# Block products for the feed-forward input projections: 44 of 88 column pairs in seven half-size products

## The chip, the core and the metric

The kernel runs on one core of a Trainium2 chip. The time is device microseconds for one execution, from a median of several runs. TensorE (PE) multiplies, VectorE (DVE) and ScalarE (ACT) work elementwise and read the PSUM banks, GpSimd (POOL) works elementwise on SBUF, SyncE (SP) issues the DMA transfers. Each engine executes its own list of instructions in order and waits for others by semaphores.

## What is computed

The reference is one step of a two-layer streaming encoder for 512 prompt frames and 64 sample frames, 576 tokens of width 1024. Each layer is feed-forward, token mixer, feed-forward, each with a modulated RMS norm in front and a gated residual behind. The change lies in the feed-forwards:

```
def _swiglu(h, w_in, w_out):                       # w_in (1024, 5632), w_out (2816, 1024)
    gate, up = jnp.split(h @ w_in, 2, axis=-1)
    return (jax.nn.silu(gate) * up) @ w_out

mod = (cond @ ada_w[l] + ada_b[l]).reshape(b, N_SUB, 3, D_MODEL)     # the modulation vectors of a layer
```

There are four feed-forwards: 0 ahead of and 1 behind the mixer of layer 0, 2 and 3 around that of layer 1. 1, 2 and 3 are called F1, F2 and F3. All is float32.

## The kernel before, in words

Tokens lie along the free dimension, in two halves of 288 (`HALF`). Features lie in partitions, 8 tiles of 128. A float32 product is made of three passes: each operand is split into a high part, its copy in the fp32r type, and a low part, the rest; a weight tile `wh`, `wl` and an activation `XH`, `XL` give wh x XH + wh x XL + wl x XH, three matmuls of 128x128 weights on 288 tokens each.

`plan` (line 49) lists the weight tiles in order of use, as pairs of blocks. A feed-forward goes in three chunks of 8, 8 and 6 column tiles (`CHUNKS`). Of each column tile j a pair holds the gate's block and the up projection's block, 8 weight tiles of 128x128 each, one DMA of 512 KB per block. After the input pairs of a chunk come its output products. `dense` (379) issues a pair: for either half of the tokens, for gate and up, 8 contraction tiles of 3 matmuls: 96 matmuls. A gate or up tile of a half has a PSUM bank of its own from a ring of four, `d`. `evac` in `ffn` (645) takes them out: silu of the gate to `sg` on ScalarE, product `hm` on VectorE, its split into `HH` (ScalarE) and `HL` (VectorE).

The weights come through a ring of three `stage` buffers. `w_prep` (364) splits a block: `wh` on ScalarE, `wl` on VectorE, each 128x1024, and then issues the transfer of the next block (`w_dma`, 354). `dense` calls it for the next pair's first block at the start of the first half and for its second block at the start of the second half, before that half's matmuls; `wh` and `wl` have rings of four.

The order of all instructions is settled while the program is written. `Model` (111) keeps rough times of the engines from fixed costs, and `Sched` (242) holds background tasks, generators that yield the time at which they are due. After every three matmuls `mm` calls `S.tick()`, which runs every task whose time has come on the model's TensorE clock (a 288-column matmul counts 123 ns there); what it issues stands in each engine's list at that place. `finish` (278) runs a task to its end at once.

`start_sub` (629) issues the first two pairs of a feed-forward, first halves first, while the norm of the second half is still worked out on VectorE, ScalarE and GpSimd. `last_pairs` (606) does the last output products, residuals and the next norm. `ada_task` (585) makes the modulation vectors of layer 1 in the background of F1 and F2: 72 tiles `aw` of 128x1024, each one DMA and two VectorE instructions `jk` with a read of the accumulator, one tile every 8500 ns of the model's clock, later if the model's VectorE is more than that ahead:

```
            for kt in range(8):
                while hold[0]:
                    yield S.clock + 1000.0
                ada_dma(pool, ahead)
                ada_tile(pool, cb, l, j, kt)
                yield max(S.clock + every, M.t["DVE"] - 1000.0)
```

Two tiles are fetched before the loop, so that two are on their way when one is read.

Of the kernel before, what the change touches and what calls it, by code (L numbers as in the profile page):

```python
# [19 lines left out]
F32 = mybir.dt.float32  # L20
# [7 lines left out]
P = 128  # L28
# [4 lines left out]
D = 1024  # L33
# [12 lines left out]
DSH = ((2, 4, 6), (1, 4, 6))  # L46


def plan():
    """The weight tiles in the order in which they are used, as pairs of blocks of up to eight 128 x 128 products;  # L50
    a tile is (source, index, rows, column)."""
# [6 lines left out]
    def ffn(f):  # L58
        for j0, nj in CHUNKS:
            for j in range(j0, j0 + nj):  # L60
                two([("in", f, tuple(range(8)), j * P), ("in", f, tuple(range(8)), FF + j * P)])
# [43 lines left out]
def outs(nk):  # L105
    """The output tiles of each pair of blocks whose sums run over nk products."""
    n = 2 if nk > 4 else (4 if nk > 2 else 8)
    return [tuple(range(m, m + n)) for m in range(0, 8, n)]


class Model:
    """Rough times of the engines, in ns, by which the background work is interleaved with the dense products."""
# [37 lines left out]
    def free(self, key, bufs):  # L150
        """When the ring's next buffer is free."""
# [73 lines left out]
class Ring:  # L225
    """A tile pool whose reuse of buffers the model sees."""
# [15 lines left out]
class Sched:  # L242
    """Interleaves the background work with the stream of dense products."""
# [45 lines left out]
def encoder_step(ctx: ExitStack, tc: tile.TileContext, a, o):  # L289
# [30 lines left out]
    # ---------------------------------------------------------------- constants  # L320
# [26 lines left out]
    # ---------------------------------------------------------------- weights  # L347
# [15 lines left out]

    def w_prep(i, g, E=None):
        if i >= len(pairs) or g >= len(pairs[i]):
            return
# [63 lines left out]

    def dense_first(evacs, feed):
        """The first two pairs of all, step by step for both halves as feed makes their inputs."""
# [36 lines left out]
    # ---------------------------------------------------------------- rsqrt, norms  # L469
# [23 lines left out]
    def norm_r(pool, halves):  # L493
        """1/rms of each token of these halves, tokens in partitions."""
# [61 lines left out]
    # ---------------------------------------------------------------- adaLN vectors  # L556
# [81 lines left out]
    def ffn(l, s, pool, task, out):  # L638
        for ci, (j0, nj) in enumerate(CHUNKS):
            HH = pool.tile([P, 8, NT], F32R, name="HH")  # L640
            HL = pool.tile([P, 8, NT], F32R, name="HL")
            for jj in range(nj):
                gate = {}

                def evac(g, half, ps, jj=jj, gate=gate):
                    t0, t1 = HALF[half]
                    if g == 0:
                        gate[half] = pool.tile([P, 288], F32, name="sg", bufs=2)
# [9 lines left out]
                elif ci == 0 and jj == 1:  # L658
                    if callable(task):
                        dense_first([ev0, evac], task)  # L660
                    else:
                        start_sub(task, [ev0, evac])
                else:
# [9 lines left out]
    # ---------------------------------------------------------------- layer 0 mixer  # L673
    def mixer0(pool, task, npool):
# [111 lines left out]
        def own(p, name, shape, at):  # L786
            """Buffers of a pair of heads; those of pair 2 lie in the residual's, which waits in DRAM."""
# [47 lines left out]
        def gdn_pair(p, kq, vt):  # L835
# [58 lines left out]
            # decay and the matrices within a block  # L894
# [20 lines left out]
            # the sample's block: both heads on the diagonal  # L915
# [20 lines left out]
        def spill(src, dst):  # L936
            """Blocks of 32 from their rows' partitions to one partition each, or back, through DRAM."""
# [34 lines left out]
            # 16 -> 32  # L972
# [18 lines left out]
            # 32 -> 64  # L991
# [19 lines left out]
            # 64 -> 128  # L1011
# [12 lines left out]
        def gdn_chunks(p, ktok, stok, nv, sc, nat, DM, PS):  # L1024
# [9 lines left out]
            # the sample's state step  # L1034
# [9 lines left out]
            # prompt: chunk by chunk  # L1044
# [68 lines left out]
            # norm of the heads' outputs, gate, back to feature-major  # L1113
# [114 lines left out]
    # ---------------------------------------------------------------- layer 1 mixer  # L1228
# [164 lines left out]
    # ---------------------------------------------------------------- the whole step  # L1393
# [13 lines left out]
    with tc.tile_pool(name="ada", bufs=1) as ap, tc.tile_pool(name="ffn", bufs=1) as fp:  # L1407
        ap, fp = Ring(M, ap), Ring(M, fp)
        crow = [ap.tile([P, D], F32, name="awp", bufs=3)[0:1] for _ in range(2)]
# [32 lines left out]
        row = ap.tile([P, D], F32, name="awp", bufs=3)[:, :P]  # L1442
# [15 lines left out]
        def scales(n):  # L1458
            """The modulation's scale for four of the feature tiles, each in a column group of its own."""
# [74 lines left out]
# columns of the packed small vectors  # L1534
# [93 lines left out]
```

## Time and profile before

| what | us |
|---|---|
| median of 3 runs | 2509.28 |
| lowest and highest run | 2495.31, 2509.33 |
| the profiled execution, first to last instruction | 2512.2 |
| F1 in the trace | about 905 to 1301 |
| F2 | about 1336 to 1731 |
| F3 | about 2095 to 2491 |

The profiled execution is one more execution; the page gives its span and nothing around it, so its span is set beside the runs' times. The profile names an instruction by engine, operation, the tiles that it writes and reads (buffer numbers left out) and their shape. Busy time is time in which at least one instruction of an engine is under way; the ends of matmuls are modelled and overlap. All instructions carry one line (188), that of the helper that issues them, so they are told apart by their tiles. PEclk is the granted TensorE clock as a share of full speed.

### The profile page before, as it was taken

To read this page: it belongs to the slowest core of one execution; us is meant where nothing else is said; L and a number is where in the kernel's file an instruction comes from. 1 tells how busy PE (TensorE), PEld (TensorE's weight loads), DVE (VectorE), ACT (ScalarE), POOL (GpSimd) and SP (SyncE) were. 2 spreads that over 40 slices of the span, in tenths; PEclk is the share of its full clock that TensorE was granted. 3 is DMA by queue.
4 is the path that set the end of the run, shared out by engine and by line. 5 is a ranking of instruction groups with operands and counts; after the bars stand their busy time and mean duration, and the time that the engine had idled before them with its cause. 6 is when DMAs were issued, how large, how long until landed. Compare 5 with 4: busy or idle time off the path is not lost.

```text
span 2512.2 us, 46274 instructions
## 1 busy us (share of the span) xinstructions
PE 2430.6 (97%) x19084; PEld 2357.9 (94%) x19084; DVE 1506.0 (60%) x2964; ACT 835.3 (33%) x1571; POOL 354.2 (14%) x599
## 2 busy tenths in 40 slices
PE   6999999999998999999999999999999999999998
PEld 5999999988888999999999999999888889999998
DVE  7677776597785666556556555535555664333334
ACT  4322212543322342122233222124655544222122
POOL 4000000341222220000021000002333332000001
PEclk8999999998877999999999999999999999999999
DMA  6555554321213144444434444322322122322222
GB/s 240 168 162 167 166 165 131 112 75 50 57 46 98 56 154 143 134 136 144 130 105 135 142 129 141 110 76 85 100 74 84 53 73 91 85 77 84 85 78 70
DMA packets 95399, 277.04 MB, mean 110 GB/s; under 512 B 24738, under 2 KB 27042, under 8 KB 94804
## 3 DMA queue, kind: packets, MB, share of 16 engines
q1 hardware_dynamic: 95188, 274.07, 34.7%
q8 instruction: 151, 2.47, 0.4%
q14 instruction: 60, 0.49, 0.1%
HBM read 262.52 MB, written 11.51 MB: 109 GB/s over the span
## 4 chain that ended last, share of the span: by engine, by line
PE 83%; DVE 10%; issue 3%; ACT 3%; POOL 2%; DMA 0%; SPq 0%; DVEq 0%; ACTq 0%; POOLq 0%
PE d L188 75%; PE a L188 8%; DVE iz L188 1%; DVE hf L188 1%; DVE cp L188 1%; POOL XL L188 1%; DVE t2k L188 1%; DVE sg L188 1%; ACT wh L188 1%; DVE sy L188 1%; POOL sn L188 1%; DVE wl L188 1%; POOL sg L188 1%; DVE raw L188 0%; ACT hf L188 0%
## 5 line engine op out<-in xcount | busy, mean ns | idle before, releaser
L188 PE MATMUL d<-XH,wh 128*128 128x288 f32 x3888 | 1176.0, 302 | 17.5 <-ACT XH L188 8.6
L188 PE MATMUL d<-XL,wh 128*128 128x288 f32 x3888 | 1158.9, 298 | 11.4 <-POOL XL L188 9.2
L188 PE MATMUL d<-XH,wl 128*128 128x288 f32 x3888 | 1155.7, 297 | 0.0
L188 PEld LDWEIGHTS d<-XH,wh 128*128 128x128 f32 x3888 | 739.3, 190 | 25.9 <-ACT XH L188 14.2
L188 PEld LDWEIGHTS d<-XL,wh 128*128 128x128 f32 x3888 | 740.1, 190 | 22.7 <-POOL XL L188 14.7
L188 PEld LDWEIGHTS d<-XH,wl 128*128 128x128 f32 x3888 | 739.6, 190 | 0.3
L188 DVE TENSOR_TENSOR wl<-stage,wh 128x1024 fp32r<-128x1024 f32 (+2 forms) x319 | 378.3, 1190 | 151.3 <-ACT wh L188 149.7
L188 ACT ACTIVATE wh<-stage 128x1024 fp32r<-128x1024 f32 (+2 forms) x345 | 348.8, 1019 | 321.1 <-PE d L188 255.1
L188 PE MATMUL d<-HH,wh 128*128 128x288 f32 x1408 | 416.3, 296 | 0.0
L188 PE MATMUL d<-HL,wh 128*128 128x288 f32 x1408 | 415.6, 295 | 0.0
L188 PE MATMUL d<-HH,wl 128*128 128x288 f32 x1408 | 414.1, 294 | 0.0
L188 DVE SCALAR_TENSOR_TENSOR jk<-aw,cb 128x1024 bf16<-128x1024 f32 x272 | 339.0, 1246 | 4.8
L188 POOL TENSOR_TENSOR acc<-acc,sq 128x288 f32<-128x288 f32 x72 | 58.7, 815 | 1613.0 <-ACT sq L188 1600.7
L188 DVE SCALAR_TENSOR_TENSOR x<-d,mod,x 128x64 f32<-128x64 f32 (+2 forms) x384 | 147.0, 412 | 220.2 <-PE d L188 218.7
L188 DVE TENSOR_TENSOR hm<-sg,d 128x288 f32<-128x288 f32 x174 | 78.9, 454 | 332.0 <-PE d L188 326.4
L188 PEld LDWEIGHTS d<-HH,wl 128*128 128x128 f32 x1408 | 264.5, 188 | 0.0
L188 PEld LDWEIGHTS d<-HL,wh 128*128 128x128 f32 x1408 | 264.2, 188 | 0.0
L188 PEld LDWEIGHTS d<-HH,wh 128*128 128x128 f32 x1408 | 264.1, 188 | 0.0
L188 ACT ACTIVATE HH<-hm 128x288 fp32r<-128x288 f32 x176 | 78.2, 444 | 545.3 <-DVE hm L188 545.3
L188 ACT ACTIVATE sg<-d 128x288 f32<-128x288 f32 x174 | 71.5, 411 | 248.1 <-PE d L188 247.8
L188 DVE TENSOR_TENSOR HL<-hm,HH 128x288 fp32r<-128x288 f32 x176 | 81.0, 460 | 90.3 <-ACT HH L188 90.3
L188 POOL TENSOR_TENSOR XL<-hf,XH 128x288 fp32r<-128x288 f32 x96 | 91.2, 964 | 83.8 <-ACT XH L188 82.9
(294 smaller groups left out, 1785.1 us busy)
## 6 DMA issues: line engine op xcount, KB each, us to landing
stage<-in_w SPq DMA_DIRECT2D x301, 512.0 KB, 3.7
aw<-in_ada SPq DMA_DIRECT2D x136, 512.0 KB, 3.5
stage<-in_w SPq DMA_DIRECT2D x36, 384.0 KB, 3.1
stage<-in_w SPq DMA_DIRECT2D x8, 320.0 KB, 2.8
x<-in_x SPq DMA_DIRECT2D x4, 576.0 KB, 7.0
xd<-x SPq DMA_DIRECT2D x1, 2304.0 KB
x<-xd SPq DMA_DIRECT2D x1, 2304.0 KB
out_k<-kf SPq DMA_DIRECT2D x8, 288.0 KB, 3.9
```

What stands on the lines that cost most here:

```text
L188: r = real(*args, **kw)
```

## The change

In 44 column pairs (12 of F1 and of F2, column tiles 10 to 21, and 20 of F3, tiles 2 to 21: `PLAIN`) the product of weights and activations is taken as a product of 2x2 blocks: gate and up, even and odd contraction tiles, first and second half of the tokens. It is made from seven products of half-size blocks (4 contraction tiles, 3 matmuls each, 288 tokens) instead of eight. Four of the seven take sums of weight blocks (`w_sum`, on VectorE), and four take sums of activation blocks (`t_task`, once for each of F1, F2 and F3), `TH` and `TL`; the sums of the products are made partly in PSUM, by accumulating on a bank whose value so far has been copied out, partly on VectorE. The weight blocks are stored with even contraction tiles first. A pair needs four `wh`/`wl` tiles instead of two, 3.5 x 1024 columns. The work after the last product of a pair (`hm`, `HH`, `HL`) is issued during the next pair (`late`). One `aw` tile is fetched ahead instead of two, in all three feed-forwards that make modulation vectors; a ring for `sg` has three buffers; some start-up buffers move. Output products, mixers, norms and feed-forward 0 stay as they are.

```diff
+PLAIN = (22, 10, 10, 2)
+EVEN_ODD = (0, 2, 4, 6, 1, 3, 5, 7)
...
+                ks = tuple(range(8)) if j < PLAIN[f] else EVEN_ODD
+                two([("in", f, ks, j * P), ("in", f, ks, FF + j * P)])
...
+    def w_split(i, src, E=V):
+        n = Model.size(src)
+        h, l = wsp.tile([P, 1024], F32R, name="wh"), wsp.tile([P, 1024], F32R, name="wl")
+        wt.setdefault(i, []).append((h, l))
+        for c in range(0, n, HB):
+            A.activation(h[:, c:c + HB], src[:, c:c + HB], AF.Copy)
+        E.tensor_sub(l[:, :n], src, h[:, :n].bitcast(F32))
+
+    def w_sum(i, n):
...
+        if n == 1:
+            V.tensor_add(x1[:, HB:], a21, a22)
+        if n == 2:
+            V.tensor_sub(x1[:, :HB], x1[:, HB:], a11)
+        if n == 3:
+            V.tensor_sub(x2[:, :HB], a11, a21)
+        if n == 4:
+            V.tensor_sub(x2[:, HB:], a12, x1[:, :HB])
+
+    def w_tile(i, n):
+        if n == 0:
+            w_split(i, st[i, 0])
+        if n == 1:
+            w_split(i, ss[i, 1])
+        if n == 2:
+            w_split(i, ss.pop((i, 3)))
...
+            w_dma()
+        if n == 3:
+            w_split(i, st[i, 1][:, HB:])
+            st.pop((i, 1))
+            w_dma()
+
     def w_prep(i, g, E=None):
...
+        if seven(i):
+            if g == 0:
+                w_sum(i, 1)
+                w_tile(i, 0)
+                w_sum(i, 2)
+            else:
+                w_sum(i, 3)
+                w_tile(i, 1)
             return
...
+    def dense7(evac):
...
+        order = (("P1", 0, x11), ("P2", 0, x21), ("P6", 1, t(2)), ("P5", 1, t(1)), ("P7", 2, t(3)), ("P3", 2, x22),
+                 ("P4", 3, t(4)))
+        bank = {}
+        for n, (name, u, xf) in enumerate(order):
+            b = {"P2": "b", "P5": "c", "P3": "c"}.get(name, "a")
...
+            for k in range(4):
+                c = c0 + k * P
+                H, L = xf(k)
+                f, e = k == 0 and name in ("P1", "P2", "P5"), k == 3
+                kw = {"skip_group_check": True}
+                T.matmul(bank[b], wh[:, c:c + P], H, start=f, stop=False, **kw)
+                T.matmul(bank[b], wh[:, c:c + P], L, start=False, stop=False, **kw)
+                T.matmul(bank[b], wl[:, c:c + P], H, start=False, stop=e, **kw)
+                S.tick()
+            evac(name, bank[b])
+            if n == 0:
+                while len(wt[i]) < 4:
+                    if len(wt[i]) == 2:
+                        w_sum(i, 4)
+                    w_tile(i, len(wt[i]))
+            if nxt7:
+                for k in {1: (1,), 2: (2,), 4: (3, 4)}.get(n, ()):
+                    w_sum(i + 1, k)
+                k = {3: 0, 5: 1, 6: 2}.get(n)
+                if k is not None:
+                    w_tile(i + 1, k)
+            elif n in (2, 4):
+                w_prep(i + 1, n // 2 - 1)
...
+    def t_task(pool):
...
+        def parts(n, k, t, E):
+            A.activation(TH[0][:, n - 1, k], t, AF.Copy)
+            E.tensor_sub(TL[0][:, n - 1, k], t, TH[0][:, n - 1, k].bitcast(F32))
+
+        new = lambda: npool.tile([P, 288], F32, name="hf", bufs=5)
+        for k in range(4):
+            e, o = 2 * k, 2 * k + 1
+            t1, b = new(), new()
+            V.tensor_sub(t1, Hf[:, e, h1], Hf[:, e, h0])
+            V.tensor_sub(b, Lf[:, e, h1], Lf[:, e, h0])
+            V.tensor_add(t1, t1, b)
+            t2 = new()
+            V.tensor_sub(t2, Hf[:, o, h1], t1)
+            V.tensor_add(t2, t2, Lf[:, o, h1])
+            yield S.clock + 300.0
+            parts(2, k, t2, V)
+            parts(1, k, t1, V)
+            t3, d = new(), new()
+            V.tensor_sub(t3, Hf[:, o, h1], Hf[:, e, h1])
+            V.tensor_sub(d, Lf[:, o, h1], Lf[:, e, h1])
+            V.tensor_sub(t2, Hf[:, o, h0], t2)
+            V.tensor_add(t2, t2, Lf[:, o, h0])
+            yield S.clock + 300.0
+            V.tensor_add(t3, t3, d)
+            parts(3, k, t3, V)
+            parts(4, k, t2, V)
+            yield S.clock + 300.0
...
         ahead = [(l, j * 8 + kt) for l, j in todo for kt in range(8)]
         ada_dma(pool, ahead)
-        ada_dma(pool, ahead)
...
+            def evac(step, ps):
+                if step == "P1":
+                    g[0] = copy("sg", ps, 3)
+                n = {"P1": 0, "P2": 1, "P6": 2}.get(step, step)
+                if step == "P6":
+                    g[1] = copy("sg", ps, 3)
+                if n in late:
+                    late.pop(n)()
+                if step == "P2":
+                    V.tensor_add(g[0], g[0], ps)
+                if step == "P5":
+                    up[0] = copy("hm", ps, 2)
+                    A.activation(g[0], g[0], AF.Silu)
+                if step == "P7":
+                    up[1] = copy("up", ps, 1)
+                if step == "P3":
+                    V.tensor_add(up[1], up[1], up[0])
+                    V.tensor_add(g[1], g[1], ps)
+                if step == "P4":
+                    A.activation(g[1], g[1], AF.Silu)
+                    products(ps)
...
                         start_sub(task, [ev0, evac])
+                    tt = S.spawn(t_task(pool)) if PLAIN[2 * l + s // 2] < 22 else None
+                elif seven(pos[0]):
+                    if tt:
+                        S.finish(tt)
+                        tt = None
+                    dense7(evac7(jj))
                 else:
                     dense(evac)
```

`products` leaves three steps in `late`: the two hm (VectorE), the two HH copies (ScalarE) and the two HL (VectorE), which the next pair's evac issues at P1, P2 and P6, or, after the last half-size pair of a chunk, `dense7` at once. `copy` is a ScalarE copy of a bank of 128x288.

## Rows read from the trace of the kernel before

**Rows 1.** Part 1 of the page: busy time of an engine in us, its share of the span, instructions.
```profile
PE 2430.6 (97%) x19084; PEld 2357.9 (94%) x19084; DVE 1506.0 (60%) x2964; ACT 835.3 (33%) x1571; POOL 354.2 (14%) x599
```

**Rows 2.** The chain of work that ended last: its shares of the span by engine, then its longest pieces within F1, F2 and F3 (start, length in us, what).
```profile
PE 83%; DVE 10%; issue 3%; ACT 3%; POOL 2%; DMA 0%; SPq 0%; DVEq 0%; ACTq 0%; POOLq 0%
...
905.27 395.35 PE d L188 x2969
...
1335.92 393.79 PE d L188 x2969
...
2094.94 395.43 PE d L188 x2981
```

**Rows 3.** Busy time of each engine in the stretches of F1, F2 and F3: stretch, its length, then busy us (and instructions) of PE, PEld (the weight loads), DVE, ACT and POOL, granted clock, DMA share and GB/s.
```profile
905.00:1301.00 396.00, 395.73 (x2976) 395.73 (x2977) 233.68 (x380) 101.88 (x160) 8.11 (x10) 1.00 0.43 136
...
1336.00:1731.00 395.00, 395.00 (x2985) 395.00 (x2986) 209.34 (x340) 101.92 (x160) 7.25 (x9) 1.00 0.38 121
...
2095.00:2491.00 396.00, 396.00 (x2991) 395.96 (x2992) 137.77 (x212) 102.50 (x162) 8.70 (x11) 1.00 0.27 79
```

**Rows 4.** Order of time in F3, all engines: start, length, engine, line, operation and tiles. 24 matmuls start from the first row to before the last; the second row is the first matmul of a next output tile, and the hm reads the bank of the tile before.
```profile
2299.75 0.29 PE L188 MATMUL d<-XH,wh 128*128 128x288 f32 x1
...
2300.95 0.29 PE L188 MATMUL d<-XH,wh 128*128 128x288 f32 x1
...
2301.22 0.45 DVE L188 TENSOR_TENSOR hm<-sg,d 128x288 f32<-128x288 f32 x1 [3.26 <-PE d L188]
...
2302.93 0.29 PE L188 MATMUL d<-XH,wh 128*128 128x288 f32 x1
```

**Rows 5.** VectorE in order of time in F1: start, length, what it did, and in brackets how long it had been idle and who released it. An hm, the hm one pair later, and between them a wl and the two jk of a modulation tile.
```profile
958.73 0.45 DVE L188 TENSOR_TENSOR hm<-sg,d 128x288 f32<-128x288 f32 x1 [3.26 <-PE d L188]
...
960.64 1.22 DVE L188 TENSOR_TENSOR wl<-stage,wh 128x1024 fp32r<-128x1024 f32 x1 [0.49 <-ACT wh L188]
961.79 1.22 DVE L188 SCALAR_TENSOR_TENSOR jk<-aw,cb 128x1024 bf16<-128x1024 f32 x1
...
963.05 1.22 DVE L188 SCALAR_TENSOR_TENSOR jk<-aw,cb 128x1024 bf16<-128x1024 f32 x1
...
971.45 0.45 DVE L188 TENSOR_TENSOR hm<-sg,d 128x288 f32<-128x288 f32 x1 [0.85 <-PE d L188]
```

**Rows 6.** Groups of instructions by form, VectorE and ScalarE: count, then busy us in all and mean ns of one, then the idle time before them.
```profile
L188 DVE TENSOR_TENSOR wl<-stage,wh 128x1024 fp32r<-128x1024 f32 x275 | 337.1, 1229 | 127.3 <-ACT wh L188 125.7 <-POOL XL L188 1.6
L188 DVE TENSOR_TENSOR HL<-hm,HH 128x288 fp32r<-128x288 f32 x176 | 81.0, 460 | 90.3 <-ACT HH L188 90.3
L188 DVE TENSOR_TENSOR cL<-ck,cH 128x512 fp32r<-128x512 f32 x8 | 5.5, 693 | 2.3 <-ACT cH L188 2.0
L188 ACT ACTIVATE sg<-d 128x288 f32<-128x288 f32 x174 | 71.5, 411 | 248.1 <-PE d L188 247.8
L188 ACT ACTIVATE cH<-ck 128x512 fp32r<-128x512 f32 x8 | 5.1, 632 | 2.2 <-DMA ck<-in_ck 2.0
```

**Rows 7.** VectorE in order of time, two small instructions of the reciprocal square root, of which the second reads the result of the first.
```profile
2062.55 0.17 DVE L188 TENSOR_SCALAR nr<-nv 96x3 int32<-96x3 int32 x1
2062.75 0.16 DVE L188 TENSOR_TENSOR nt<-nr 96x3 f32<-96x3 f32 x1
```

**Rows 8.** ScalarE in order of time in F1, the copy HH and the next wh.
```profile
959.22 0.45 ACT L188 ACTIVATE HH<-hm 128x288 fp32r<-128x288 f32 x1 [3.29 <-DVE hm L188]
959.57 1.04 ACT L188 ACTIVATE wh<-stage 128x1024 fp32r<-128x1024 f32 x1
```

**Rows 9.** Part 6 of the page, DMA transfers: count, size, median us from issue to landing.
```profile
stage<-in_w SPq DMA_DIRECT2D x301, 512.0 KB, 3.7
aw<-in_ada SPq DMA_DIRECT2D x136, 512.0 KB, 3.5
```

**Rows 10.** SP's queue in order of time in feed-forward 0, two transfers of modulation tiles with one of a weight block between them: start, length of the issue, what.
```profile
203.54 0.33 SPq L312 DMA_DIRECT2D aw<-in_ada  x1
...
211.37 0.33 SPq L312 DMA_DIRECT2D aw<-in_ada  x1
```

**Rows 11.** VectorE in order of time at the end of the first two pairs of F3: the last hm and HL of the second pair, and the next weight block's wl.
```profile
2103.94 0.45 DVE L188 TENSOR_TENSOR hm<-sg,d 128x288 f32<-128x288 f32 x1 [2.04 <-PE d L188]
2104.91 0.46 DVE L188 TENSOR_TENSOR HL<-hm,HH 128x288 fp32r<-128x288 f32 x1 [0.51 <-ACT HH L188]
2105.86 1.23 DVE L188 TENSOR_TENSOR wl<-stage,wh 128x1024 fp32r<-128x1024 f32 x1 [0.49 <-ACT wh L188]
```

**Rows 12.** TensorE in stretches around a gap ahead of F3: stretch, length, busy us (instructions), granted clock, DMA share, GB/s.
```profile
2072.00:2074.00 2.00, 0.41 (x2) 0.84 0.75 256
2074.00:2076.00 2.00, 2.00 (x9) 0.50 0.68 260
2076.00:2078.00 2.00, 2.00 (x14) 0.81 0.00 0
2078.00:2080.00 2.00, 2.00 (x21) 1.00 0.07 16
```

**Rows 13.** The modulation tiles' instructions alone (jk and the reads of its accumulator, four records a tile) in stretches of F1 and F2: stretch, length, VectorE's busy us (records), granted clock, DMA share, GB/s.
```profile
905.00:1055.00 150.00, 36.88 (x60) 0.99 0.44 140
...
1586.00:1636.00 50.00, 9.83 (x16) 1.00 0.31 95
1636.00:1686.00 50.00, 0.00 (x0) 1.00 0.26 75
```

More of the change, by code (lines that the diff above doesn't have):

```diff
@@ L362, in w_dma, with seven @@
                                                 ap=[[n, P], [1, n]]))
+    def seven(i):
+        return i < len(pairs) and pairs[i][0][0][2] == EVEN_ODD
+    ss = {}
+    spool = [None]
+    HB = 4 * P
+    def w_split(i, src, E=V):
[6 more added lines that the diff above has]
+    def w_sum(i, n):
+        g0, g1 = st[i, 0], st[i, 1]
+        a11, a12, a21, a22 = g0[:, :HB], g0[:, HB:], g1[:, :HB], g1[:, HB:]
+        if n in (1, 3):
+            ss[i, n] = spool[0].tile([P, 1024], F32, name="ss", bufs=2)
+        x1, x2 = ss[i, 1], ss.get((i, 3))
+        if n == 1:
[13 more added lines that the diff above has]
+            w_split(i, ss.pop((i, 3)))
+            ss.pop((i, 1))
+            st.pop((i, 0))
+            w_dma()
[3 more added lines that the diff above has]
+            w_dma()
     def w_prep(i, g, E=None):
         if i >= len(pairs) or g >= len(pairs[i]):
+            return
+        if seven(i):
[6 more added lines that the diff above has]
+                w_tile(i, 1)
             return
@@ L429, in dense @@
                         evacs[q](g, half, ps[g])
+    TH, TL = {}, {}
+    def dense7(evac):
+        i = pos[0]
+        pos[0] += 1
+        nxt7 = seven(i + 1)
+        h0, h1 = slice(0, 288), slice(288, 576)
+        x11 = lambda k: (XH[:, 2 * k, h0], XL[:, 2 * k, h0])
+        x21 = lambda k: (XH[:, 2 * k + 1, h0], XL[:, 2 * k + 1, h0])
+        x22 = lambda k: (XH[:, 2 * k + 1, h1], XL[:, 2 * k + 1, h1])
+        t = lambda n: lambda k: (TH[0][:, n - 1, k], TL[0][:, n - 1, k])
+        order = (("P1", 0, x11), ("P2", 0, x21), ("P6", 1, t(2)), ("P5", 1, t(1)), ("P7", 2, t(3)), ("P3", 2, x22),
[3 more added lines that the diff above has]
+            b = {"P2": "b", "P5": "c", "P3": "c"}.get(name, "a")
+            if b not in bank:
+                bank[b] = psum.tile([P, 512], F32, name="a")[:, :288] if b == "b" else psum.tile([P, 288], F32, name="d")
+            wh, wl = wt[i][u]
+            c0 = HB if name in ("P2", "P5", "P3") else 0
+            for k in range(4):
[21 more added lines that the diff above has]
+                w_prep(i + 1, n // 2 - 1)
+        if not nxt7:
+            for n in (0, 1, 2):
+                evac(n, None)
+        wt.pop(i)
@@ L638, in ffn, with evac7, products, mul @@
     def ffn(l, s, pool, task, out):
+        spool[0] = pool
+        tt = None
+        late = {}
+        def evac7(jj):
+            g, up = {}, {}
+            t0s = HALF[0][0], HALF[1][0]
+            HHc, HLc = HH, HL
+            def products(ps):
+                hm = {}
+                def mul():
+                    for half in (1, 0):
+                        hm[half] = pool.tile([P, 288], F32, name="hm", bufs=2)
+                        V.tensor_mul(hm[half], g[half], up[1] if half else ps)
+                def high():
+                    for half in (1, 0):
+                        A.activation(HHc[:, jj, t0s[half]:t0s[half] + 288], hm[half], AF.Copy)
+                def low():
+                    for half in (1, 0):
+                        r = slice(t0s[half], t0s[half] + 288)
+                        V.tensor_sub(HLc[:, jj, r], hm[half], HHc[:, jj, r].bitcast(F32))
+                late.update({0: mul, 1: high, 2: low})
+            def copy(name, ps, bufs):
+                t = pool.tile([P, 288], F32, name=name, bufs=bufs)
+                A.activation(t, ps, AF.Copy)
+                return t
+            def evac(step, ps):
[19 more added lines that the diff above has]
+                    products(ps)
+            return evac
         for ci, (j0, nj) in enumerate(CHUNKS):
@@ L647, in evac @@
                     if g == 0:
-                        gate[half] = pool.tile([P, 288], F32, name="sg", bufs=2)
+                        gate[half] = pool.tile([P, 288], F32, name="sg", bufs=3)
                         A.activation(gate[half], ps, AF.Silu)
@@ L1408, in encoder_step @@
         ap, fp = Ring(M, ap), Ring(M, fp)
-        crow = [ap.tile([P, D], F32, name="awp", bufs=3)[0:1] for _ in range(2)]
+        first = fp.tile([P, 4, 4, 288], F32, name="TH").rearrange("p a b c -> p (a b c)")
+        crow = [first[0:1, g * D:(g + 1) * D] for g in range(2)]
         for g in range(2):
@@ L1441, in encoder_step @@
         cb = ap.tile([P, 2, D], F32, name="cb")
-        row = ap.tile([P, D], F32, name="awp", bufs=3)[:, :P]
+        row = first[:, 2 * D:2 * D + P]
         G.memset(row, 0.0)
```

12 lines of the change are left out of this document (8 added, 4 removed).

## Prediction

> **What bounds the kernel now.** I read the totals first, then the chain that ended last, then the three feed-forwards stage by stage, then single instructions. The totals show TensorE busy 97% of the span, VectorE 60%, ScalarE 33% [rows 1]. The chain is 83% TensorE, and within the three feed-forwards that change (F1, F2, F3 below) it is one unbroken piece of TensorE work of about 395 us each [rows 2]. So there the end is set by how many matmuls are issued and by nothing else. VectorE is busy 59% of F1, 53% of F2 and 35% of F3 [rows 3]. The matmuls start 3.18 us / 24 = 0.1325 us apart [rows 4], although each shows 0.29 us: only the spacing counts. A column pair of 96 takes 12.72 us, which is also the distance from an hm to the second next of VectorE [rows 5].
>
> **What is removed.** A pair takes 7 products of 12 matmuls instead of 96 matmuls: 84 x 0.1325 = 11.13 us, 1.59 us less. For 12 + 12 + 20 = 44 pairs that is -70.0 us, if the saved places are not filled by waits. One product is 1.59 us.
>
> **VectorE within a pair.** The price of an instruction is the distance to the next start. A 1024-wide wl starts at 960.64 and the jk after it at 961.79: 1.15 us for a duration of 1.22 [rows 5], so independent neighbours overlap by 0.07 to 0.08. The by-form groups give 0.46 us for 288 elements, 0.69 for 512, 1.23 for 1024 [rows 6]; I charge 0.38, 0.61, 1.15. Where one needs the result of the one before, nothing overlaps: 0.17 long, 0.20 apart [rows 7].
> Before: two hm, two HL, two wl = 4 x 0.38 + 2 x 1.15 = 3.82 us per pair. After: seven of 288 (two hm, two HL, three additions of partial products), five of 512 (four weight sums, the last wl), three wl of 1024 = 2.66 + 3.05 + 3.45 = 9.16 us, against 11.13 of TensorE. VectorE also has to wait for ScalarE in two places. The wl of the next pair's first tile stands behind ScalarE's copy of P5, a silu and two half-tile wh copies, some 1.9 us (0.35 from start to start for 288 [rows 8], 0.54 and 0.63 for 512 [rows 6]), of which VectorE's own work covers all but 0.95. The third tile's wl stands behind add, silu and two copies, 0.5 us uncovered. The floor is 9.16 + 1.45 = 10.6 us, below 11.13: without further work VectorE keeps up and the 26 pairs without modulation work (six in F2, twenty in F3) run at 11.13.
> The Trainium skill, "VectorE: DVE Perf Modes", section "The DRAIN you can't avoid", says that the next VectorE instruction doesn't start until the pipe of the one before has emptied; by that the whole durations would count, and VectorE would bind these 26 pairs too. The overlap of wl and jk speaks against it here.
> ScalarE has about 6.5 us per pair and does not bind. The copies that free a PSUM bank for the next accumulation (P1 before P6, P6 before P7, P7 before P4, P5 before P3) start some 0.27 us after the next product has begun [rows 4, 5] and take 0.41 [rows 6], each under a whole product of 1.59 us: nothing, unless ScalarE is 0.9 us late. A stage transfer lands 3.7 us after issue [rows 9] and has some 5 us between the last reader of its buffer and the first weight sum that needs it: nothing. The modulation tiles, now fetched one ahead instead of two, follow each other 7.8 us apart even in feed-forward 0 [rows 10] and land after 3.5 us [rows 9]: nothing.
>
> **The sums of the activations (t_task).** Per k: 14 VectorE instructions of 288 = 5.3 us, four dependent steps at 0.11 more, two waits of 0.5 us for a ScalarE copy: 6.9 us, 27.8 us for four k. It is spawned when the first two pairs are done, and in F1 and F2 its twelve steps are due 300 ns apart on the planner's clock, which ticks after every three matmuls: all twelve are put into the queues during pair 2, ahead of that pair's hm and of pair 3's second weight tile. Let E be the end of pair 1. By the same place in F3 of before, VectorE ends its HL at E+1.7 and the next wl at E+3.4 [rows 11]. Then 27.8 us of sums, to E+31.2; hm, HH and the wh copy of pair 3's second block on ScalarE (1.04 [rows 8]) to E+33.1; its wl to E+34.3. TensorE has four banks, which are pair 2; it can start pair 3's first tile when the sg of pair 2, also queued behind the sums, is out, but the third matmul of pair 3's second tile, nominally at E+16.2, needs that wl. Stall: 34.3 - 16.2 = 18.1 us, twice.
> In F3 the first half-size pair is pair 2 itself, so the whole task is finished before it. TensorE does P1 and P2, to E+3.2; P6 accumulates on P1's bank, whose copy stands on ScalarE behind the last copies of the task, E+29.0, so P6 starts at E+29.5: 26.3 us. From both sides: nothing of the 18.1 if the steps are spread over six pairs, 27.8 if nothing is covered; in F3 20 (only the last T2 awaited) to 31.
> After an idle stretch the clock is at half: after the gap at 2072 it reads 0.50 and 0.81 in the next two 2 us slices, then 1.00 [rows 12]. That costs some 2 us for each of three stalls, 6 us (0 to 10).
>
> **The modulation tiles in F1 and F2.** They are 2.52 us of VectorE each (two jk, 1.26 from start to start [rows 5]) and come every 10 us: 15 per 150 us; they end near 1620, in the third quarter of F2 [rows 13]. So 12 pairs of F1 and six of F2 carry them. A pair of length t then needs t = 9.16 + 0.252 t + uncovered waits. With no uncovered wait t = 12.25, with all 1.45 us t = 14.2. These tiles are put in by clock and sometimes fill a wait, so I take half: t = 13.2, 2.1 above 11.13 and 0.5 above the 12.72 of before. 18 x 2.1 = 38, less some 3 us that TensorE is ahead at the start of each of three runs of six: +29 us (13 to 57). In the plain pairs of before this work hid in VectorE's idle time.
> The last pair of each of seven runs ends in silu, hm, HH, HL, some 1.7 us, and the output product needs it 2 to 2.8 us in: 2 us together for unlucky ones.
>
> **Sum.** -70.0 + 2 x 18.1 + 26.3 + 6 + 29 + 2 = +29.5 us: the span 2512.2 becomes 2541.7. The profiled execution is 2.9 us above the median of the runs, 2509.28, so I predict 2539 us. Averages hide this: F1's VectorE work would rise from 234 to about 326 us in 396, still less than full; the loss is in the bursts and in the runs of six.
>
> **Rivals.**
> 1. The modulation tiles fit into the waits: VectorE then stays just under TensorE also in F1 and F2. For it: the planner delays a tile when its own VectorE time is ahead. Against: it does so only by more than its interval. Its sum is -70 + 62.5 + 6 + 2 = +0.5: 2510 us, no change.
> 2. The other side, faster: the twelve steps of t_task in F1 and F2 go out over six or more pairs, where VectorE has 12.72 - 3.82 - 3.2 = 5.7 us free in each; it decides at 27.8 / 5.7 = 4.9 pairs. Then 36.2 us and two clock losses vanish, and the modulation costs its low end: -70 + 26.3 + 2 + 13 + 2 = -26.7, 2483 us. Against: 300 ns is less than one tick.
> 3. VectorE's instructions don't overlap in the dependent order of the new pair, and whole durations count: 7 x 0.46 + 5 x 0.69 + 3 x 1.23 = 10.4 us [rows 6], with the waits of 1.45 a floor of 11.8, which is 0.7 above 11.13. That is 26 x 0.7 = +18 us; the modulation tiles are then 2.66 us per 10, and their pairs take (10.4 + 0.7) / 0.734 = 15.1 us, 18 x 1.9 = +34 over the forecast: 2590 us. For it: many new steps read what the one or two before wrote. Against: the overlap in the rows. It is what the page of the Trainium skill named above would lead to.
>
> **How the numbers follow.** About 1% is what a measurement of this kernel tells from no change: faster means below 2484, slower above 2534. Forecast 0.45, within 2520 to 2560 (0.31 slower, 0.14 same); rival 1 0.20 (0.19 same, 0.01 faster); rival 2 0.15 (0.12 faster, 0.03 same); rival 3 0.14 slower; the rest 0.06 (0.01 faster, 0.03 same, 0.02 slower). Together 0.14 faster, 0.39 same, 0.47 slower. The range 2482 to 2580 reaches rival 2 and stops short of the whole of rival 3.
>
> **What would show it.** Per half-size pair 48 matmuls read TH or TL and 36 instead of 96 read XH or XL: 2112 new ones, 2640 gone, 528 fewer in all. The pairs of F3 from its second half-size one on should be 11.1 us apart; if they are above 11.5, rival 3. After the first two pairs of F1 and F2 VectorE should show an unbroken block of some 28 us and TensorE a gap or gaps of about 18 us in all, in F3 one of about 26, with a clock of 0.50 behind it; without the gaps in F1 and F2, rival 2. The runs of six in F1 should take 13 us per pair with VectorE over 95% busy; at 11.1 to 11.5 it is rival 1. F3 as a whole should come out 4 us shorter, F1 20 and F2 10 longer. I am wrong altogether if VectorE's sums cost less than the start-to-start distances say, or are queued elsewhere.

## The result, and the profile after

The changed kernel takes 2548.82 us (median of 4 runs, 2535.52 to 2550.91), the kernel before 2509.31 beside it: 1.015 times as long, 95% interval 1.0113 to 1.0186. That is slower, though by less than 2%; it lies within the range of the prediction and 10 us above its 2539. The profiled span grew from 2512.2 to 2549.2, by 37.0 us.

In most kernels of this study the executions lie in two groups some 13 us apart (before: 2494 to 2502 and 2508 to 2518), and in the one profile of a lower group, that of "HL on GpSimd and hf", mixer 0 ran at a higher granted clock (0.95 instead of 0.91 from 475 to 710 us) and F1 began 12 us earlier. So beside the medians stands "F1 to the end": the stretch from F1's last wait for the norm to the end of the profiled execution. It is 1606.9 us before (from 905.27 [rows 2]) and 1647.6 after (from 901.57), +40.7.

Part 1 of the page after, then its chain by engine, answering to [rows 1, 2]:

```profile
PE 2384.6 (94%) x18556; PEld 2304.2 (90%) x18556; DVE 1791.0 (70%) x3528; ACT 986.8 (39%) x2015; POOL 353.6 (14%) x599
...
PE 70%; DVE 19%; ACT 5%; issue 3%; POOL 2%; DMA 1%; SPq 0%; DVEq 0%; ACTq 0%; POOLq 0%
```

528 matmuls are gone, as meant. But VectorE has 19% of the chain instead of 10%: TensorE's work is no longer one piece in F1, F2 and F3. The windows (columns as in [rows 3]) of F1, F2 and F3, of a run of pairs with modulation tiles and of a run without:

```profile
902.00:1324.00 422.00, 389.33 (x2820) 384.37 (x2819) 319.67 (x552) 143.33 (x284) 7.61 (x9) 0.96 0.39 130
1360.00:1769.00 409.00, 385.11 (x2827) 382.10 (x2827) 286.17 (x494) 144.18 (x284) 7.26 (x9) 0.97 0.35 115
2135.00:2527.00 392.00, 366.36 (x2740) 365.85 (x2741) 259.68 (x448) 169.83 (x358) 8.62 (x11) 0.97 0.26 80
1097.00:1156.00 59.00, 48.97 (x349) 47.24 (x350) 53.76 (x92) 28.22 (x65) 0.00 (x0) 0.99 0.41 141
2186.00:2231.00 45.00, 45.00 (x342) 45.00 (x341) 37.13 (x61) 26.73 (x61) 0.00 (x0) 1.00 0.31 95
```

F1 needs 422 us instead of 396, F2 409 instead of 395, F3 392 instead of 396. TensorE's idle places are in few spots. TensorE in order of time, the gaps of the burst in F1, one of a run with modulation tiles and the one of F3 (in brackets the idle time and what ended it):

```profile
922.79 0.29 PE L191 MATMUL d<-XH,wl 128*128 128x288 f32 x1
930.77 0.61 PE L191 MATMUL d<-XH,wh 128*128 128x288 f32 x1 [7.69 <-ACT sg L191]
...
942.95 0.61 PE L191 MATMUL d<-XH,wh 128*128 128x288 f32 x1 [6.25 <-ACT wh L191]
943.36 0.44 PE L191 MATMUL d<-XL,wh 128*128 128x288 f32 x1
944.22 0.61 PE L191 MATMUL d<-XH,wl 128*128 128x288 f32 x1 [0.41 <-DVE wl L191]
...
1125.58 0.40 PE L191 MATMUL d<-TH,wh 128*128 128x288 f32 x1 [2.08 <-ACT sg L191]
...
2172.59 0.61 PE L191 MATMUL d<-TH,wh 128*128 128x288 f32 x1 [25.64 <-ACT sg L191]
```

The first row is the last matmul ahead of a gap. Most others name ScalarE, but its copies were queued behind VectorE's work: the sg for which TensorE waits at 930.77 stands behind a TH copy that had waited 2.77 us for VectorE.

```profile
929.65 0.78 ACT L191 ACTIVATE TH<-hf 128x288 fp32r<-128x288 f32 x2 [2.77 <-DVE hf L191]
930.33 0.39 ACT L191 ACTIVATE sg<-d 128x288 f32<-128x288 f32 x1
```

VectorE, and one copy of ScalarE, in the same places: the sums of the activations from their first to their last instruction, with pair 2's hm and the next block's wl behind them, then a part of a run with modulation tiles:

```profile
913.52 0.45 DVE L191 TENSOR_TENSOR hf<-XH 128x288 f32<-128x288 f32 x1
...
940.29 0.83 DVE L191 TENSOR_TENSOR TL<-hf,TH 128x288 fp32r<-128x288 f32 x2 [0.51 <-ACT TH L191]
941.03 0.45 DVE L191 TENSOR_TENSOR hm<-sg,d 128x288 f32<-128x288 f32 x1
...
942.93 1.23 DVE L191 TENSOR_TENSOR wl<-stage,wh 128x1024 fp32r<-128x1024 f32 x1 [0.49 <-ACT wh L191]
...
1115.78 0.82 DVE L191 TENSOR_TENSOR HL<-hm,HH 128x288 fp32r<-128x288 f32 x2
1116.33 0.41 ACT L191 ACTIVATE hm<-d 128x288 f32<-128x288 f32 x1 [1.25 <-DVE HL L191]
1116.52 0.68 DVE L191 TENSOR_TENSOR ss<-ss,stage 128x512 f32<-128x512 f32 x1
1118.14 1.23 DVE L191 TENSOR_TENSOR wl<-stage,wh 128x1024 fp32r<-128x1024 f32 x1 [0.94 <-ACT wh L191]
1119.28 1.22 DVE L191 SCALAR_TENSOR_TENSOR jk<-aw,cb 128x1024 bf16<-128x1024 f32 x1
```

The granted clock behind three gaps (columns as in the windows above), answering to [rows 12], and F3's pairs in the chain of waits, where a pair is a piece of 12 matmuls and one of 72:

```profile
932.00:934.00 2.00, 2.00 (x10) 2.00 (x9) 1.46 (x5) 0.78 (x2) 0.00 (x0) 0.50 0.00 0
...
1155.00:1157.00 2.00, 2.00 (x11) 2.00 (x10) 2.00 (x4) 1.70 (x4) 0.00 (x0) 0.50 0.21 68
...
2174.00:2176.00 2.00, 2.00 (x10) 2.00 (x10) 1.94 (x3) 0.62 (x3) 0.00 (x0) 0.50 0.72 209
```

```profile
2185.16 1.60 PE a L191 x12
2186.76 9.53 PE d L191 x72
2196.29 1.60 PE a L191 x12
2197.89 9.53 PE d L191 x72
2207.41 1.60 PE a L191 x12
```

### The profile page after: what moved, and what is told of

Its sections match the earlier page's. It is cut to its first block, busy times and chain, and to the rows that moved or that the text cites. A ratio compares the mean times of both kernels' runs of the same rounds, so it can differ in the third digit from the quotient of the medians.

```text
span 2549.2 us, 46027 instructions
## 1 busy us (share of the span) xinstructions
PE 2384.6 (94%) x18556; PEld 2304.2 (90%) x18556; DVE 1791.0 (70%) x3528; ACT 986.8 (39%) x2015; POOL 353.6 (14%) x599
## 4 chain that ended last, share of the span: by engine, by line
PE 70%; DVE 19%; ACT 5%; issue 3%; POOL 2%; DMA 1%; SPq 0%; DVEq 0%; ACTq 0%; POOLq 0%
PE d L191 61%; PE a L191 9%; DVE hf L191 3%; DVE wl L191 3%; DVE jk L191 2%; ACT wh L191 2%; DVE iz L191 1%; DVE ss L191 1%; DVE sg L191 1%; DVE cp L191 1%; ACT sg L191 1%; DVE TL L191 1%; DVE t2k L191 1%; DVE sy L191 1%; POOL sn L191 1%
## 5 line engine op out<-in xcount | busy, mean ns | idle before, releaser
L191 PE MATMUL d<-XH,wh 128*128 128x288 f32 x2832 | 869.8, 307 | 47.6 <-ACT sg L191 16.1
L191 PE MATMUL d<-XL,wh 128*128 128x288 f32 x2832 | 850.9, 300 | 16.1 <-POOL XL L191 9.5
L191 PE MATMUL d<-XH,wl 128*128 128x288 f32 x2832 | 847.7, 299 | 0.8 <-DVE wl L191 0.8
L191 PEld LDWEIGHTS d<-XL,wh 128*128 128x128 f32 x2832 | 545.3, 193 | 23.2 <-POOL XL L191 15.2
L191 PEld LDWEIGHTS d<-XH,wl 128*128 128x128 f32 x2832 | 544.3, 192 | 1.7 <-DVE wl L191 1.5
L191 DVE TENSOR_TENSOR wl<-stage,wh 128x1024 fp32r<-128x1024 f32 (+3 forms) x319 | 354.9, 1117 | 169.4 <-ACT wh L191 167.8
L191 ACT ACTIVATE wh<-stage 128x1024 fp32r<-128x1024 f32 (+3 forms) x389 | 334.6, 878 | 274.4 <-PE d L191 240.9
L191 PE MATMUL d<-TH,wh 128*128 128x288 f32 x704 | 214.2, 304 | 46.9 <-ACT sg L191 46.9
L191 PE MATMUL d<-TL,wh 128*128 128x288 f32 x704 | 212.4, 302 | 0.0
L191 PE MATMUL d<-TH,wl 128*128 128x288 f32 x704 | 212.1, 301 | 0.0
```

The costliest lines, as they stand in the source:

```text
L191: r = real(*args, **kw)
```

## The experiments

The theory was that three separate things eat the 70 us: the sums put into the queues in one burst in F1 and F2, the same burst in F3 with nothing beside it, and VectorE's work per pair where modulation tiles come on top. The rivals: a cost that every half-size pair carries; waits for ScalarE or for a buffer in place of VectorE's work. All ratios are to the kernel before, run on the same chip beside each kernel (medians there 2508.3 to 2511.1 us).

| kernel | us | ratio (95%) | F1 to the end |
|---|---|---|---|
| before | 2509.3 | | 1606.9 |
| after | 2548.8 | 1.015 (1.0113 to 1.0186) | 1647.6 |
| sums spread | 2518.9 | 1.0069 (1.0038 to 1.0099) | 1614.4 |
| F3 alone | 2505.5 | 0.9998 (0.9967 to 1.003) | 1603.1 |
| modulation tiles held back | 2520.6 | 1.008 (1.0052 to 1.0108) | 1614.0 |
| HL on GpSimd | 2549.8 | 1.0193 (1.0152 to 1.0234) | 1643.5 |
| HL left out | 2529.0 | 1.0084 (1.0054 to 1.0115) | 1623.7 |
| P5 copied to hf | 2528.7 | 1.0093 (1.0058 to 1.0127) | 1637.3 |
| HL on GpSimd and hf | 2548.7 | 1.0184 (1.0122 to 1.0246) | 1646.5 |
| spread and held back | 2473.4 | 0.9862 (0.9816 to 0.9907) | 1569.4 |
| the same, F3 from pair 10 | 2458.3 | 0.979 (0.9736 to 0.9844) | 1553.3 |
| eight plain pairs each | 2460.0 | 0.9798 (0.9741 to 0.9855) | 1553.6 |
| the fastest: F3 from pair 6 | 2449.8 | 0.9744 (0.9698 to 0.979) | 1547.4 |

**Sums spread.** In `t_task`, three times:

```diff
-            yield S.clock + 300.0
+            yield S.clock + 5000.0
```

> Only the pace of t_task changes: its steps are due 5000 ns apart instead of 300, so in F1 and F2 they spread over about five pairs (F3, which finishes the task at once, keeps its gap of 26 us). Theory (the loss at the start of F1 and F2 is the placing of 27.5 us of VectorE work in one go): the TensorE gaps there, 15.0 and 15.2 us, and the half-clock matmuls behind them, 3.9 and 4.1 us, go; 2549 - 38 = 2511 us, 2505 to 2520. Rival (VectorE has no room left in F1 and F2 at all, with the modulation tiles in every pair): the same us come back as short waits in the pairs, 2535 to 2550.

2518.9 us, and 33.2 us less from F1 to the end. The gaps of 15 us each in F1 and F2 shrink to these and two like them in F2 (TensorE in order of time):

```profile
982.41 0.40 PE L191 MATMUL d<-XH,wh 128*128 128x288 f32 x1 [1.20 <-ACT wh L191]
983.67 0.40 PE L191 MATMUL d<-XH,wl 128*128 128x288 f32 x1 [0.72 <-DVE wl L191]
```

At the bursts, which had cost 38.2 us with the half clock behind them (below), 4.9 us of gaps and some 3 us of half clock are left. In the three runs of six pairs the gaps grew by 3 us and the half clock behind them shrank by 6. So the burst is a matter of when the sums are issued, not of their amount.

**F3 alone.**

```diff
-PLAIN = (22, 10, 10, 2)
+PLAIN = (22, 22, 22, 2)
```

> Half-size products in F3 only (20 pairs); F1 and F2 are plain. Theory (pairs without modulation tiles run at TensorE's 11.13 us, and F3 pays one gap): 20 x -1.59 + 25.8 + 2.9 of clock = -3 against the kernel before, 2506 us, 2500 to 2510. Rival (something shared costs: one modulation tile fetched ahead instead of two, moved start-up buffers, rings): above 2513, with the loss ahead of F3.

As expected; from F1 to the end 3.8 us less than before. In F3 the 31.8 us of removed matmuls pay for the one gap, the half clock behind it and nothing else, so there is no hidden cost per half-size pair.

**Modulation tiles held back.** A flag is set while half-size pairs run; elsewhere the tiles come more often:

```diff
-                while hold[0]:
+                while hold[0] or quiet[0]:
...
-        at = S.spawn(ada_task(ap, cb, [(1, j) for j in range(9)], 8500.0))
+        at = S.spawn(ada_task(ap, cb, [(1, j) for j in range(9)], 5600.0))
```

> t_task as in the change; the modulation tiles pause while half-size pairs are issued and are due every 5600 ns instead of 8500 elsewhere in F1 and F2. Theory (the six-pair runs of F1 and F2 are slow because modulation tiles take VectorE there): all these pairs at 11.13 us, so the 30.2 us of gaps and some 8 us of half clock behind them go: 2511 us; up to 2525 if the denser tiles cost something in the plain pairs. Rival (ScalarE's order of copies causes the gaps, not VectorE's load): gaps at the same places, 2540 or more.

2520.6 us, 33.6 less from F1 to the end. The runs of six have no gap within them any more; the chain in F1, then the window:

```profile
1101.58 9.53 PE d L191 x72
1112.71 9.53 PE d L191 x72
```

```profile
1089.00:1146.00 57.00, 57.00 (x432) 57.00 (x432) 46.22 (x74) 34.36 (x77) 0.00 (x0) 1.00 0.31 103
```

Two pieces begin 11.13 us apart, and VectorE is busy 46.2 of 57 us. The bursts got 5.5 us longer.

**HL on GpSimd.** In `low`, the step of `late` that makes HL: `V.tensor_sub(HLc...)` becomes `G.tensor_sub(HLc...)`.

> The two HL subtractions of each half-size pair run on GpSimd instead of VectorE. Theory (VectorE's load decides in the six-pair runs with modulation tiles): 0.76 us less VectorE work per pair, 0.76 / 0.748 = 1.0 us per pair, 18 pairs: -18 us, 2531; the pairs without modulation stay at 11.13. Rival (the waits come from the order of ScalarE's copies): within 4 us of 2549. Third: GpSimd at work slows VectorE's instructions, and the pairs of F3 lengthen: above 2555.

A miss: the median did not move, and F1 to the end is 4.1 us shorter where 18 were expected. The groups by form, then VectorE's two sums while GpSimd works (1129.35 to 1131.64), and a jk beside the next pair's subtractions:

```profile
L191 POOL TENSOR_TENSOR HL<-hm,HH 128x288 fp32r<-128x288 f32 x88 | 96.3, 1114 | 1038.9 <-ACT HH L191 1038.9
L191 DVE TENSOR_TENSOR ss<-stage 128x512 f32<-128x512 f32 x88 | 67.1, 762 | 4.1 <-DMA stage<-in_w 4.1
L191 DVE TENSOR_TENSOR ss<-ss,stage 128x512 f32<-128x512 f32 x44 | 41.2, 936 | 1.1
```

```profile
1130.04 0.93 DVE L191 TENSOR_TENSOR ss<-stage 128x512 f32<-128x512 f32 x1
1131.00 1.19 DVE L191 TENSOR_TENSOR ss<-ss,stage 128x512 f32<-128x512 f32 x1
...
1143.09 1.83 DVE L191 SCALAR_TENSOR_TENSOR jk<-aw,cb 128x1024 bf16<-128x1024 f32 x1
```

Both groups of sums had a mean of 686 ns in the after kernel. The two sums of this pair take 0.24 + 0.50 = 0.74 us longer, and 0.76 had been saved. In the three runs of six 23.9 us of gaps are left (30.2 before the edit), and at the ends of the runs 10.5 us are new, where the output product waits for HH and HL. The third theory has its mechanism but not its time: the pairs of F3 stay 11.13 us apart.

ScalarE's copy of P5 waits for HL too: it goes into the ring hm, whose two buffers hold the hm of the pair before until HL has read them. A third buffer found no room (87.875 KB per partition wanted, 87.0625 left), so three other runs tell VectorE's time from this wait.

**HL left out.** The half-size pairs' `low` does nothing, and the output products read HH for HL.

> The HL subtractions of the half-size pairs are left out, and the output products read HH where they would read HL (a part of the computation is left out; as many matmuls as in the after kernel). VectorE has two instructions of 0.38 us less per pair and GpSimd nothing more, and the wait of the P5 copy for HL is gone too. Theory, VectorE's work decides: a pair with modulation tiles shortens by 0.76 / 0.748 = 1.0 us, 18 us of the 30 us of gaps, and most of the half-clock stretches of 8 us behind them go with the shorter gaps: 2525 to 2533. The bursts stay. If so, what ate the gain of the GpSimd version is GpSimd itself (its 1.1 us per subtraction, and VectorE's longer sums beside it). Rival, ScalarE's order of copies decides and not VectorE: no more than the ring alone gives, 2541 or more.

2529.0 us, 23.9 less from F1 to the end: gaps of 15 us in the three runs instead of 30.2, and no half clock behind them. Taking 0.76 us of VectorE's time away without giving GpSimd anything pays what I had expected of the GpSimd version. But this run also ends the wait for the buffer; the next one ends that wait alone.

**P5 copied to hf.**

```diff
-                    up[0] = copy("hm", ps, 2)
+                    up[0] = npool.tile([P, 288], F32, name="hf", bufs=5)
+                    A.activation(up[0], ps, AF.Copy)
```

> ScalarE copies P5 into a buffer of the ring hf, which the finished sums have left free, instead of the ring hm: that copy no longer waits until both HL of the pair before have been read. Nothing else is changed. Theory, VectorE's work per pair decides: the four gaps that end on this copy (1.8 us each, 7 us in all) go, and the gaps at sg grow by about as much; 23 to 30 us of gaps in the three runs, 2541 to 2549. Rival, the ring decides and what was saved by leaving HL out was its wait: 14 us of gaps fewer as there, and 2529 to 2535.

Mixed. The median, 2528.7, is where the rival put it, but the five runs spread from 2526.0 to 2542.4, and the profiled one took 2539.5. Its trace shows the theory's picture: the copy no longer waits, the gaps that ended on it are gone, and 27.4 us of gaps are left (30.2 before the edit), now all at sg:

```profile
1109.89 0.40 PE L191 MATMUL d<-TH,wh 128*128 128x288 f32 x1 [0.52 <-ACT sg L191]
1114.78 0.40 PE L191 MATMUL d<-TH,wh 128*128 128x288 f32 x1 [1.44 <-ACT sg L191]
1124.21 0.40 PE L191 MATMUL d<-TH,wh 128*128 128x288 f32 x1 [1.22 <-ACT sg L191]
```

From F1 to the end it gains 10.3 us, some 7 more than its gaps. Its longest gap is shorter (1.97 us between two starts, for 2.65), and no half-clock stretch follows, which neither theory had counted. Without HL 12 us of gaps went beyond this, so VectorE's time sets most of them, and this wait few.

**HL on GpSimd and hf.** Both edits.

> HL of the half-size pairs on GpSimd, and P5's copy in a buffer of hf, so that nothing waits for the slower HL but the output product. Theory, VectorE gives back what it saves: beside a GpSimd subtraction its two sums took 0.93 and 1.19 us instead of 0.69, 0.74 us together, and two jk 1.83 and 1.71 instead of 1.22, against 0.76 us saved per pair. Then the profiled span is that of the run with hf alone, 2538 us, within 6 us (2532 to 2544), with gaps of 23 to 32 us in the three runs. Rival, the gain was lost to the wait for the buffers of hm: without it the span comes near that of the run without HL, 2527 us (under 2531), with some 16 us of gaps.

The profiled span, 2535.4 us, lies where the theory put it, but by luck: F1 began at 888.9 us there, 11 us earlier than with hf alone. From F1 to the end it needs 1646.5 us, 9.2 more than with hf alone and 22.8 more than without HL. So the buffer was not what took the gain: the rival falls. The gaps at the ends of the three runs with modulation tiles, where the output product waits for HH and HL, are 7 us more, with 3 us of half clock behind them, and at the ends of the four other runs 3 us more; within the three runs only 4 us of gaps were gained, where leaving HL out gained 12 more than hf alone. So GpSimd costs twice: VectorE's sums beside it, and a late HL at the end of each run.

**Both cures together.** Sums 10 us apart, modulation tiles held back.

> Both edits of the two runs before together: the twelve steps of t_task are due 10 us apart instead of 0.3, and the modulation tiles are put in only while the pairs are plain, one every 5.6 us there. Theory A, the bursts and the crowded runs are separate losses: the after kernel loses 38 us to the bursts of F1 and F2 with the half clock behind them and 38 us to gaps and half clock within the runs of six, so 2549 - 76 = 2473 us; the two edits alone gave 30 and 28, which by themselves make 2491. I expect 2480 (2468 to 2495). Rival B, VectorE is simply full: a plain pair of F1 now holds 3.82 us of its own, 27.8 / 9.4 = 3.0 of sums and 12.72 / 5.6 x 2.52 = 5.7 of modulation, 12.5 of 12.72 us, and waits of 0.5 to 1.5 us per pair come back there: 20 pairs x 1 = 20 us, 2493 to 2505. F3 is unchanged in both: a gap of about 26 us.

2473.4 us: the two losses are separate, and rival B is false at this density. It had VectorE busy for 12.5 of 12.72 us, 98%, in a plain pair of F1; in F1 ahead of the half-size pairs (plain pairs and output products, with sums and modulation tiles beside them) the trace has 83%, and TensorE has no gap:

```profile
905.00:1060.00 155.00, 155.00 (x1164) 155.00 (x1163) 128.69 (x232) 43.52 (x76) 0.00 (x0) 0.99 0.45 160
```

**F3's pairs from the tenth on**, `PLAIN = (22, 10, 10, 10)`:

> The same, and in F3 the half-size pairs begin after ten plain ones instead of two, so that the sums there also lie beside plain pairs: 8 fewer half-size pairs (8 x 1.59 = 12.7 us back), and the gap of 25.8 us with its 2.9 us of half clock gone. Theory A: 16 us below the run before, some 2464 us (2452 to 2480), and no TensorE gap over 3 us in F3. Rival B: the gap comes back as waits for VectorE in F3's plain pairs; they hold 3.82 + 3.0 of 12.72 us there, so B has little to stand on; it would give the same time as the run before or 5 us more.

16.1 us less from F1 to the end, as worked out, and F3 begins as one piece in the chain:

```profile
2061.04 163.24 PE d L191 x1229
2224.28 1.60 PE a L191 x12
2225.88 9.53 PE d L191 x72
```

**Eight plain pairs**, `PLAIN = (22, 8, 8, 8)`, sums 7 us and tiles 4.8 us apart:

> Half-size pairs after eight plain ones in F1, F2 and F3, the sums 7 us apart, the modulation tiles every 4.8 us while pairs are plain. Six pairs more than in the run before: theory A, -6 x 1.59 = -9.5 us, some 2455 us (2442 to 2472). Rival B: a plain pair of F1 would hold 3.82 + 27.8 / 6.6 = 4.2 + 12.72 / 4.8 x 2.52 = 6.7, together 14.7 us of VectorE in 12.72, so the runs' waits come back in the plain pairs: 8 pairs of F1 x 2 us = +16, slower than the run before by some 6 us.

Between the two: no gain, but no loss of 6 us either. Of the 9.5 us 7.7 went into waits for wh and wl, 5.5 in plain pairs of F1 and F2 (two of these rows below, F2) and 2.2 at the end of a run:

```profile
1398.01 0.41 PE L191 MATMUL d<-XH,wh 128*128 128x288 f32 x1 [0.99 <-ACT wh L191]
1399.27 0.40 PE L191 MATMUL d<-XH,wl 128*128 128x288 f32 x1 [0.72 <-DVE wl L191]
```

**F3 from the sixth pair**, `PLAIN = (22, 10, 10, 6)`, F3's sums 4 us apart:

> The fastest version so far (sums 10 us apart, modulation tiles outside the half-size runs, ten plain pairs in F1 and F2), with the half-size pairs of F3 beginning after six plain pairs instead of ten and its sums 4 us apart. Theory, a plain pair of F3 has room: 3.82 + 27.8 / 3.8 = 11.1 of 12.72 us, no modulation tiles there; four more half-size pairs give -4 x 1.59 = -6.4 us, some 2452 us. Rival, with the sums' waits for ScalarE that is already too dense, as where eight pairs had to hold sums and tiles: gaps of 5 us or more in F3's plain pairs and no gain, 2458 or more.

5.9 us less from F1 to the end; at 2449.8 us it beats both kernels, 2.6% below the one before.

## Why the prediction was right

It had the verdict, and most of its terms hold one by one. Too small are the half clock and, mostly through it, the runs with modulation tiles. TensorE's gaps below are sums over what exceeds 0.1325 us between two starts.

| term | forecast | measured |
|---|---|---|
| 528 matmuls | -70.0 | -70.0 (pairs 11.13 apart) |
| bursts in F1 and F2 | +36.2 | +30.2 (15.0 and 15.2) |
| gap in F3 | +26.3 | +25.8 |
| half clock behind these | +6 | +10.9 |
| runs with modulation tiles | +29 | +30.2 (11.7, 8.2, 10.3) |
| half clock behind their gaps | 0 | +8 |
| run ends | +2 | +0.5 |

That makes +35.6 of the +40.7 from F1 to the end. Some 4 us more are 40 single matmuls in the runs with modulation tiles that start 0.08 to 0.16 us late, about half of them directly behind a gap; 1 us I could not place. The 3.7 us of difference to the spans' +37.0 arose ahead of F1.

- **The sums in one block.** Forecast 27.8 us of VectorE, measured 913.52 to 941.03, 27.5 (the parts named in the forecast add up to 6.8 us per k and 27.0, not 6.9 and 27.8); the wl of pair 3's second block ends at E + 34.0 (E is 910.2), forecast E + 34.3. TensorE's three gaps are 3.1 us short of 18.1 because 2.5 us of that stall appear as matmuls at half clock between them; that belongs to the clock's term, which is therefore too high in the table by as much as this one is too low. Gaps and clock of the three bursts together: 66.9, forecast 68.5.
- **The modulation tiles.** The gaps, 30.2 us, lie on the forecast of 29, but the term was meant to be all that these 18 pairs lose, and with the half clock and the single late matmuls that is 42. Half of the uncovered waits was a choice, and its bounds of 13 and 57 do not follow from the figures beside them, which give 11 (no wait, 3 us off per run) to 55 (all waits, nothing off). These pairs follow each other 11.1 to 15.0 us apart (first matmul on TH), 13.6 on average, where I took 13.2. I expected VectorE over 95% busy there; it is 91% (53.76 of 59 us). The rest is waits for ScalarE, such as the 0.94 us ahead of the wl at 1118.14: ScalarE's copy of P5 stands there until HL has been read from its buffer. Giving the copy another buffer moved the gaps and removed 3 us of them; taking 0.76 us from VectorE as well halved them. So VectorE's time decides, and the waits set where the gaps lie.
- **The mis-sized term is the clock.** I charged 2 us for each of three stalls. TensorE also dropped to 0.50 behind five of the six gaps of 2.4 to 2.7 us between two starts within the runs, 1.5 to 1.6 us each time (not behind the one that ends at 1125.58). How many drops there are is not settled by the gaps: the kernel with the sums spread has the same six, and the clock fell behind one of them. The last gap of F1's first run, after (where it fell, see 1155.00 above) and with the sums spread (where it stayed at 1.00):

```profile
1153.64 0.40 PE L191 MATMUL d<-TH,wh 128*128 128x288 f32 x1 [2.37 <-ACT sg L191]
...
1142.66 0.40 PE L191 MATMUL d<-TH,wh 128*128 128x288 f32 x1 [2.37 <-ACT sg L191]
1144.00:1146.00 2.00, 2.00 (x17) 2.00 (x17) 2.00 (x4) 2.00 (x4) 0.00 (x0) 1.00 0.12 43
```

- **Rival 1 and 2** fell in this kernel, but rival 2 is what the spread version makes true: its mechanism was right, and the place of the steps decides. Its time, 2483 us, was not reached (2518.9), because the runs with modulation tiles still have 33 us of gaps there.
- **Rival 3** is out. The pairs of F3 are 11.13 us apart, where it needed 11.8. The rows show why: a wl of 1.23 us at 1118.14 is followed by a jk after 1.14 us. The Trainium skill, "VectorE: DVE Perf Modes", section "The DRAIN you can't avoid", lets the next instruction start only when the pipe of the one before has emptied, but adds that one that is not held starts earlier. The trace agrees with the addition: this jk starts 0.09 us before the wl has ended. The forecast's reading of the section left the addition out, and without it the section would lead to this rival.
- **By stage**: from F1's start to F2's +27.8 (forecast +20), F2 with mixer 1 +15.9 (+10), F3 to the end -2.9 (-4). The excess over the forecast is mostly the clock.

## What to carry to other kernels

When an engine's average load after a change is still under 100%, look at where its new work is queued: here TensorE ran without a gap beside a VectorE at 83% when its work was spread, and the same work in bursts of 27.5 us, together with half-size pairs on top of another background task, cost more than seven products for eight had saved. Background work should be due at a spacing worked out from the free time per step, and kept out of the steps that have none left. A gap's price is its length and what the clock loses behind it, and the second part can differ for the same gap.

## What the hardware showed unexpectedly

- VectorE instructions became longer while GpSimd subtracted 288 fp32 columns (1.11 us each on GpSimd, 0.46 on VectorE): sums of 512 columns 0.93 and 1.19 instead of 0.69, a jk 1.83 and 1.71 instead of 1.22. The 61 sums of the first kind with no such subtraction beside them stayed at 0.69, the 27 others took 0.94 on average. Moving 0.76 us per pair away left the median where it was.
- The granted clock was 0.50 for some 3 us (1.5 to 1.6 us lost) behind five of six gaps of TensorE of 2.4 to 2.7 us between two starts, 1.2 GHz instead of 2.4, and behind one of the same six with the sums spread. Behind the gaps of up to 1.97 us in the run with hf only the first matmul was slow, by 0.1.
- The page's median from issue to landing of the modulation tiles rose from 3.5 to 4.4 us, with one tile fetched ahead instead of two. That is not a slower transfer: 29 of the 49 landings that the trace before tells lie in feed-forward 0 or ahead of it, 17 of the 19 after in F1 and F2, and in F1 and F2 alone both medians are 4.4. VectorE was idle 4.8 us in all ahead of these tiles.
